# The lo parts of the plain feed-forward weight blocks by an accumulating DMA

## The chip, the cores and the metric

The kernel runs on one core of one Trainium2 chip. The metric is the device time of one launch in microseconds (us). The kernel before was timed in three runs. One further execution was recorded by the profiler; all durations in this document come from such recorded executions.

## The reference

The kernel computes one layer of an encoder on 512 tokens of width 1024, in float32. Only the end of the layer bears on the change:

```python
gates = jax.nn.sigmoid(gate_pre.reshape(B, S, N_BRANCHES, D_MODEL))
merged = (gates[:, :, 0] * (y_pool @ w_up_pool[l]) + gates[:, :, 1] * (y_attn @ w_up_attn[l])
          + gates[:, :, 2] * (y_rec @ w_up_rec[l]))
x = x + merged @ w_out[l]
h2 = rms_norm(x, norm2_g[l])
gu = h2 @ w_ffn_in[l]                     # (512, 1024) @ (1024, 2 * 2816)
x = x + (jax.nn.silu(gu[..., :FFN_HIDDEN]) * gu[..., FFN_HIDDEN:]) @ w_ffn_out[l]
```

Ahead of it stand a combined input projection, a pooling mixer, differential attention and a gated recurrence; behind it a last norm. The changed lines work in `h2 @ w_ffn_in` alone.

## The kernel before, in words

**Two-part numbers.** TensorE reads its operands in a shorter format (F32R). So every float32 operand w is split into hi, which is w rounded to that format, and lo = w - hi, and a product is made of three terms: hi x hi, hi x lo and lo x hi. For a weight block, `split_w` makes hi with a cast on ScalarE (line 183) and lo with a subtraction on VectorE (line 184). Both go into tiles `whi` and `wlo` of the pool `wsp`, which has three buffers for each name. A fourth split therefore waits until TensorE has read the buffer of the first.

**Feed-forward input.** The 2 x 2816 columns are worked off as 22 pairs of 128 columns, pair j being block j of the "up" half and block j of the "gate" half. Pair 0 is done plainly. Pairs 1 to 21 use Strassen's scheme in Winograd's form: a pair is a 2 x 2 arrangement of blocks, and 7 products stand in for 8. Of a pair's weights four *parts* are made, in this order:

- part 0: the first block as it stands, 128 x 1024 (`split_w`, the plain block);
- parts 1 and 2: sums of blocks (`sums`, three additions on VectorE, lines 261 to 265), split into `shi` and `slo` of another pool (lines 300 and 302);
- part 3: the second half of the second block as it stands, 128 x 512 (`split_w` again).

`ffn_pair_bodies` has the four bodies that use them: `first` (two products with part 0), `second` and `third` (two products each, with parts 1 and 2) and `fourth` (one product with part 3). Each product is 12 matmuls of 256 columns: four with hi, four with hi against the lo of the activations, four with lo. Its sums stand in PSUM banks `mm` and `rc`; ScalarE copies `mm` to `u` after the first product (line 1246) and again after the third (line 1264), VectorE makes the gate sum `g` (line 1275), ScalarE its silu (lines 1278 and 1285), and VectorE the result `hid` (line 1286). The product after a copy accumulates into the same bank, so it waits for the copy.

**Loads and order.** A pair's raw weights, 2 x 512 KB, are loaded by two DMAs of SyncE's queue into `raw` of the pool `wraw`, which has two buffers; so pair j + 2 is loaded when all that reads the raw weights of pair j is done. `Jobs.pump` writes loads and splits ahead of their use, up to four splits. A scheduler then sets the order on each engine; TensorE's order is fixed as written. Nothing else but these queues sets the order: each engine takes its instructions in turn and waits at the head for semaphores.

GpSimd (POOL) computes the few reciprocal roots of the norms and, in the feed-forward input, nothing.

Of the kernel before, what the change touches and what calls it, by code (L numbers as in the profile page):

```python
# [11 lines left out]
F32 = mybir.dt.float32  # L12
F32R = mybir.dt.float32r
U8 = mybir.dt.uint8
AF = mybir.ActivationFunctionType
ALU = mybir.AluOpType
PSUM = bass.MemoryType.PSUM

P = 128
# [3 lines left out]
KT = D // P  # L23
HEADS = 4
FFN = 2816
FT = FFN // P
# [50 lines left out]
def encoder_kernel(ctx: ExitStack, tc: tile.TileContext, x, norm1_g, w_in, pool_w, pool_scale,  # L77
# [3 lines left out]
    nc = tc.nc  # L81
# [82 lines left out]
    class Part:  # L164
# [9 lines left out]
        def split(self):  # L174
            self.hi, self.lo = split_w(self.view(self.chunk.raw), self.a, self.b, self.wpool, self.skip)
            self.chunk.left -= 1

    def split_w(view, a, b, wpool=None, skip=0):

        n, k = a * b, skip // 4  # L180
        hi, lo = ((wpool or wsp).tile([P, n if wpool else 1088], F32R, name=name)[:, k:k + n]
                  .rearrange("p (a b) -> p a b", a=a) for name in ("whi", "wlo"))
        nc.scalar.copy(out=hi, in_=view)  # L183
        LAST["wlo"] = nc.vector.tensor_tensor(out=lo, in0=view, in1=hi.bitcast(F32), op=ALU.subtract).ins  # L184
        return hi, lo

# [88 lines left out]
    class PairPart:  # L275

        wpool = None
# [15 lines left out]
        def sums_and_split(self):  # L293
            k = KT // 2
            if self.which in (1, 2):
                if self.chunk.sums is None:
                    self.chunk.add()
                view = self.chunk.sums[:, 2:4] if self.which == 1 else self.chunk.sums[:, 0:2]
                hi = LAST["ws"].tile([P, 2, k * P], F32R, name="shi")
                nc.scalar.copy(out=hi, in_=view)  # L300
                lo = LAST["ws"].tile([P, 2, k * P], F32R, name="slo")
                on_dve = nc.vector.tensor_tensor(out=lo, in0=view, in1=hi.bitcast(F32), op=ALU.subtract).ins  # L302
                FF.setdefault(f"s12_{self.chunk.name}", (on_dve,))
            elif self.which == 0:
                hi, lo = split_w(self.chunk.raw[:, 0], KT, P, None, self.skip)
                hi, lo = (t.rearrange("p k c -> p (k c)").rearrange("p (n x) -> p n x", n=2) for t in (hi, lo))
            else:
                hi, lo = split_w(self.chunk.raw[:, 1, k:], k, P, None, self.skip)
                hi, lo = (t.rearrange("p k c -> p (k c)").rearrange("p (n x) -> p n x", n=1) for t in (hi, lo))
            self.hi, self.lo = (t.rearrange("p n (k c) -> p n k c", c=P) for t in (hi, lo))  # L310
            self.chunk.left -= 1
# [237 lines left out]
    class First:  # L549
        wpool = None  # L550
# [51 lines left out]
    for i in range(3):  # L602
        for n, _ in enumerate(cols_mm(ps0[i], first[i], hT, KT, 0, 0, 256, i == 0)):
            if (i, n) in ((1, 5), (2, 5)):
                b = 1 + i
# [607 lines left out]
    class TilePart:  # L1213

        wpool = None
# [545 lines left out]
```

## Time and profile before

| | us |
|---|---|
| time, median of 3 runs (lowest to highest) | 885.27 (884.33 to 885.49) |
| the profiled execution's own time | 883.61 |
| its span, first to last instruction | 881.8 |
| PE (TensorE matmuls) busy | 869.9 |
| DVE (VectorE) busy | 658.6 |
| ACT (ScalarE) busy | 441.8 |
| POOL (GpSimd) busy | 19.0 |
| SyncE's DMA packets, share of the 16 DMA engines' span | 31.9% |

How to read it: the difference between span and time (1.8 us) lies around the first and the last instruction. Matmuls are pipelined, so a busy PE may still be one that could be fed faster. Idle time of an engine counts only where something that sets the end waits for it. In the rows, a line such as `L184` is that of the kernel before; `wlo<-raw,whi` means that the instruction reads `raw` and `whi` and writes `wlo`.

### The profile page before, as it was taken

The page shows a single profiled execution, that of the slowest core. Times are in us where ns is not written, and L with a number is a line of the kernel's source. Part 1 is how long each engine was busy: PE and PEld are TensorE (multiplying, and loading weights), DVE is VectorE, ACT ScalarE, POOL GpSimd, SP SyncE. Part 2 cuts the span into 40 slices and gives each one's busy share as a digit, 9 for nine tenths or more (in the row PEclk, how much of TensorE's full clock was granted, in tenths as well). Part 3 has the DMA queues.
Part 4 walks back from the last instruction along what each step waited for, and adds up shares of the span by engine and source line. Part 5 has one row for each costly group of instructions (what it writes and reads, how often), then busy time and mean ns, then how long its engine had stood idle before and what let it go on. Part 6 is the DMA issues. An engine that isn't in the chain of part 4 may idle for free.

```text
span 881.8 us, 13804 instructions
## 1 busy us (share of the span) xinstructions
PE 869.9 (99%) x5604; PEld 784.7 (89%) x5604; DVE 658.6 (75%) x992; ACT 441.8 (50%) x696; POOL 19.0 (2%) x35
## 2 busy tenths in 40 slices
PE   8999999999999999999999999999999999999996
PEld 7989988888998888888999898999999999988885
DVE  6788664845859765788777655997888888747996
ACT  6544333434646583444355425755555555533563
POOL 1000000000000000000000001000000000000001
PEclk9999999999999999999999999999999999999999
DMA  7330113124134114222431760153433443355002
GB/s 242 96 120 25 49 48 110 35 73 138 46 95 141 49 48 155 96 86 58 144 96 48 262 192 1 49 143 97 134 105 96 130 110 97 120 190 191 2 0 96
DMA packets 109579, 88.52 MB, mean 100 GB/s; under 512 B 2742, under 2 KB 98508, under 8 KB 109388
## 3 DMA queue, kind: packets, MB, share of 16 engines
q1 hardware_dynamic: 108924, 86.59, 31.9%
q8 instruction: 44, 0.72, 0.3%
q10 hardware_dynamic: 592, 1.05, 0.3%
q14 instruction: 19, 0.16, 0.1%
HBM read 85.54 MB, written 2.10 MB: 99 GB/s over the span
## 4 chain that ended last, share of the span: by engine, by line
PE 91%; DVE 4%; DMA 2%; issue 1%; ACT 1%; POOL 0%; SPq 0%; POOLq 0%; DVEq 0%; ACTq 0%
PE mm L90 62%; PE rc L90 25%; PE tp L90 2%; PE tp L98 2%; DMA raw<-in_w_out_dram 1%; DMA raw<-in_w_in_dram 1%; DVE wlo L184 1%; DVE hid L354 1%; DVE flo L354 1%; DMA xin<-in_x_dram 0%; DVE hrow L455 0%; DVE h_lo L472 0%; PE rc L98 0%; DVE slo L302 0%; DVE sums L261 0%
## 5 line engine op out<-in xcount | busy, mean ns | idle before, releaser
L183 ACT CAST whi<-raw 128x1024 fp32r<-128x1024 f32 (+1 forms) x134 | 128.7, 968 | 142.5 <-PE mm L90 98.7
L184 DVE TENSOR_TENSOR wlo<-raw,whi 128x1024 fp32r<-128x1024 f32 (+1 forms) x134 | 148.9, 1117 | 50.6 <-ACT whi L183 32.1
L90 PE MATMUL mm<-hT_hi,wlo 128*128 128x512 f32 (+1 forms) x380 | 92.3, 375 | 0.2 <-DVE wlo L184 0.2
L90 PE MATMUL mm<-hT_hi,whi 128*128 128x512 f32 (+1 forms) x380 | 91.6, 376 | 0.0
L90 PE MATMUL mm<-hT_lo,whi 128*128 128x512 f32 (+1 forms) x380 | 90.7, 374 | 0.0
L90 PEld LDWEIGHTS mm<-hT_lo,whi 128*128 128x128 f32 x380 | 66.6, 189 | 11.5
L90 PEld LDWEIGHTS mm<-hT_hi,whi 128*128 128x128 f32 x380 | 66.4, 189 | 11.7 <-ACT hT_hi L468 0.4
L90 PEld LDWEIGHTS mm<-hT_hi,wlo 128*128 128x128 f32 x380 | 66.2, 188 | 11.6 <-DVE wlo L184 0.4
L302 DVE TENSOR_TENSOR slo<-sums,shi 128x1024 fp32r<-128x1024 f32 x52 | 63.2, 1218 | 0.1
L300 ACT CAST shi<-sums 128x1024 fp32r<-128x1024 f32 x52 | 54.7, 1053 | 3.0 <-DVE sums L264 2.5
L261 DVE TENSOR_TENSOR sums<-raw 128x1024 f32<-128x1024 f32 x26 | 31.6, 1217 | 3.6 <-DMA raw<-in_w_in_dram 3.5
L860 DVE TENSOR_TENSOR kq<-kq,pyr 128x256 f32<-128x256 f32 x48 | 18.2, 420 | 18.3 <-PE rc L90 18.3
L90 PE MATMUL rc<-kq,kc 128*128 128x128 f32 x224 | 31.6, 284 | 0.0
L90 PEld LDWEIGHTS rc<-kq,kc 128*128 128x128 f32 x224 | 30.1, 191 | 1.5
L1002 ACT ACTIVATE s<-s,mx 128x512 f32<-128x512 f32 x32 | 23.1, 721 | 15.6 <-DVE mx L1000 15.4
L829 ACT COPY kc<-kq 128x512 f32<-128x512 f32 x28 | 18.6, 665 | 20.2 <-PE rc L90 12.6
L1275 DVE TENSOR_TENSOR g<-mm,g 128x256 f32<-128x256 f32 x21 | 8.9, 423 | 23.7 <-PE mm L90 23.7
L90 PE MATMUL mm<-y_hi,whi 128*128 128x512 f32 x96 | 26.6, 395 | 0.0
L90 PE MATMUL mm<-fhi,slo 128*128 128x256 f32 x168 | 26.1, 277 | 0.5 <-DVE slo L302 0.4
L90 PE MATMUL mm<-y_lo,whi 128*128 128x512 f32 x96 | 26.4, 393 | 0.0
L90 PE MATMUL mm<-fhi,shi 128*128 128x256 f32 x168 | 26.0, 277 | 0.1
L90 PE MATMUL mm<-y_hi,wlo 128*128 128x512 f32 x96 | 26.1, 391 | 0.0
(377 smaller groups left out, 1983.1 us busy)
## 6 DMA issues: line engine op xcount, KB each, us to landing
raw<-in_w_ffn_in_dram SPq DMA_DIRECT2D x44, 512.0 KB, 5.3
raw<-in_w_in_dram SPq DMA_DIRECT2D x34, 512.0 KB, 4.2
raw<-in_w_in_dram SPq DMA_DIRECT2D x13, 1024.0 KB, 5.2
raw<-in_w_ffn_out_dram SPq DMA_DIRECT2D x7, 1024.0 KB, 4.8
raw<-in_w_out_dram SPq DMA_DIRECT2D x4, 1024.0 KB, 9.6
xin<-in_x_dram SPq DMA_DIRECT2D x4, 512.0 KB, 4.1
raw<-in_w_up_rec_dram SPq DMA_DIRECT2D x2, 1024.0 KB
raw<-in_w_up_pool_dram SPq DMA_DIRECT2D x2, 1024.0 KB, 4.9
```

Source lines behind the costliest of these rows:

```text
L90: i = nc.tensor.matmul(out_, lhsT=lhsT, rhs=rhs, start=start, stop=stop, skip_group_check=chain)
L98: tc.keep_in_program_order(nc.tensor.transpose(out_, in_, idn))
L183: nc.scalar.copy(out=hi, in_=view)
L184: LAST["wlo"] = nc.vector.tensor_tensor(out=lo, in0=view, in1=hi.bitcast(F32), op=ALU.subtract).ins
L261: nc.vector.tensor_tensor(out=strided(sums, 0, [[2 * half, 2], [1, half]]), in0=strided(self.raw, 0, [[3 * half, 2], [1, half]]), in1=stri ...
L300: nc.scalar.copy(out=hi, in_=view)
L302: on_dve = nc.vector.tensor_tensor(out=lo, in0=view, in1=hi.bitcast(F32), op=ALU.subtract).ins
L354: last[0] = form(**kw).ins
L829: nc.scalar.copy(out=strided(kc, 0, [[2 * n, S // (2 * n)], [n, 2], [1, n]]), in_=strided(kq, 2 * S, [[2 * n, S // (2 * n)], [S + n, 2], [ ...
L860: nc.vector.tensor_tensor(out=xv, in0=xv, in1=tv, op=ALU.mult)
L1002: nc.scalar.activation(out=s, in_=s, func=AF.Exp, scale=-1.0, bias=mx[:, c:c + 1], accum_out=zz[:, i, c:c + 1])
L1275: on_dve = nc.vector.tensor_tensor(out=c["g"], in0=c["x"], in1=c["g"], op=ALU.add).ins
```

## The change

For pairs 5 to 21 the lo part of parts 0 and 3 is no longer subtracted on VectorE. ScalarE writes -hi into `wlo`, and a DMA of GpSimd's queue then adds the raw weights onto it in SBUF. Pairs 1 to 4, the sums of parts 1 and 2 and all other splits stay as they are.

```diff
-    def split_w(view, a, b, wpool=None, skip=0):
+    def split_w(view, a, b, wpool=None, skip=0, by_dma=False):
 
         n, k = a * b, skip // 4
         hi, lo = ((wpool or wsp).tile([P, n if wpool else 1088], F32R, name=name)[:, k:k + n]
                   .rearrange("p (a b) -> p a b", a=a) for name in ("whi", "wlo"))
         nc.scalar.copy(out=hi, in_=view)
+        if by_dma:
+            nc.scalar.activation(out=lo, in_=hi.bitcast(F32), func=AF.Copy, scale=-1.0)
+            nc.gpsimd.dma_start(out=lo.bitcast(F32), in_=view, accum_op=ALU.add)
+            return hi, lo
         LAST["wlo"] = nc.vector.tensor_tensor(out=lo, in0=view, in1=hi.bitcast(F32), op=ALU.subtract).ins
         return hi, lo
...
             elif self.which == 0:
-                hi, lo = split_w(self.chunk.raw[:, 0], KT, P, None, self.skip)
+                hi, lo = split_w(self.chunk.raw[:, 0], KT, P, None, self.skip, self.chunk.name in range(5, FT))
                 hi, lo = (t.rearrange("p k c -> p (k c)").rearrange("p (n x) -> p n x", n=2) for t in (hi, lo))
             else:
-                hi, lo = split_w(self.chunk.raw[:, 1, k:], k, P, None, self.skip)
+                hi, lo = split_w(self.chunk.raw[:, 1, k:], k, P, None, self.skip, self.chunk.name in range(5, FT))
```

That takes 34 subtractions from VectorE (17 of 128x1024, 17 of 128x512) and gives 34 instructions to ScalarE and 34 DMAs to GpSimd's queue. The order on TensorE and on SyncE's queue is the same as before. Line numbers behind the new lines are 4 higher.

On ScalarE, one pair in the steady part of the stage (`silu<-mm` is line 1285 before and 1289 after, the first `u<-mm` behind it the copy of line 1246 before and 1250 after) before:

```order
L183 CAST whi<-raw 128x1024
L1285 ACTIVATE silu<-mm 128x256
L1246 COPY u<-mm 128x256
L183 CAST whi<-raw 128x512
L1264 COPY u<-mm 128x256
```

The same place on ScalarE after the change, where `wlo<-whi` writes -hi:

```order
L183 CAST whi<-raw 128x1024
L1289 ACTIVATE silu<-mm 128x256
L185 ACTIVATE wlo<-whi 128x1024
L1250 COPY u<-mm 128x256
L183 CAST whi<-raw 128x512
L185 ACTIVATE wlo<-whi 128x512
L1268 COPY u<-mm 128x256
```

The longer new instruction stands between `silu` and the copy of `mm` that TensorE waits for; the shorter one stands behind the second cast.

On VectorE, the same stretch of one pair before (`sums` are the block sums of parts 1 and 2):

```order
L302 TENSOR_TENSOR slo<-sums,shi 128x1024
L184 TENSOR_TENSOR wlo<-raw,whi 128x1024
L261 TENSOR_TENSOR sums<-raw 128x2x512
L1286 TENSOR_TENSOR hid_5326<-silu,u 128x512
L184 TENSOR_TENSOR wlo<-raw,whi 128x512
L264 TENSOR_TENSOR sums<-sums,raw 128x512
L265 TENSOR_TENSOR sums<-sums,raw 128x512
```

And on VectorE after the change:

```order
L306 TENSOR_TENSOR slo<-sums,shi 128x1024
L265 TENSOR_TENSOR sums<-raw 128x2x512
L1290 TENSOR_TENSOR hid_5326<-silu,u 128x512
L268 TENSOR_TENSOR sums<-sums,raw 128x512
L269 TENSOR_TENSOR sums<-sums,raw 128x512
```

The two subtractions are gone and what stood behind them moves up; nothing else changes its place. The matmuls that read `wlo` now wait for the DMA, and SyncE's load of pair j + 2 waits for both accumulating DMAs of pair j as well, since they read its raw weights.

## Prediction

> **What bounds the kernel now.** I read the page first (busy times, chain), then a table by stretches of the stage that changes, then who waits there, then one pair in order of time, and last the DMAs.
>
> ```profile
> span 881.8 us, 13804 instructions
> PE 869.9 (99%) x5604; PEld 784.7 (89%) x5604; DVE 658.6 (75%) x992; ACT 441.8 (50%) x696; POOL 19.0 (2%) x35
> ...
> PE 91%; DVE 4%; DMA 2%; issue 1%; ACT 1%; POOL 0%; SPq 0%; POOLq 0%; DVEq 0%; ACTq 0%
> ```
>
> TensorE is busy 99% of the span and makes up 91% of the chain that ended last. VectorE's 4% of the chain must be looked for where the change is. The feed-forward input of pairs 5 to 21 lies at about 594 to 762 us; its table by stretches (columns: PE, PEld, DVE, ACT, POOL busy, granted clock, DMA share, GB/s), with the stage behind it as a fourth row:
>
> ```profile
> 594.00:650.00 56.00, 56.00 (x494) 55.91 (x494) 47.30 (x59) 32.39 (x54) 0.00 (x0) 1.00 0.42 114
> 650.00:706.00 56.00, 56.00 (x496) 56.00 (x496) 47.74 (x60) 32.37 (x53) 0.00 (x0) 1.00 0.40 112
> 706.00:762.00 56.00, 56.00 (x496) 56.00 (x495) 47.49 (x59) 32.20 (x54) 0.00 (x0) 1.00 0.39 115
> 762.00:800.00 38.00, 38.00 (x172) 31.55 (x171) 22.81 (x21) 15.46 (x18) 0.00 (x0) 1.00 0.43 155
> ```
>
> PE is busy 56.00 of 56.00 us in all three stretches, at full clock. VectorE is busy 142.5 of 168 us and ScalarE 97.0. In the list of waits of 594 to 762 us no row of its twelve has PE waiting; the others wait for PE:
>
> ```profile
> DVE g L1275 <- PE mm L90: 23.3, 17, 1.8
> ...
> ACT u L1246 <- PE mm L90: 8.2, 17, 0.5
> ACT whi L183 <- PE mm L90: 4.3, 17, 0.3
> ...
> DVE wlo L184 <- ACT whi L183: 0.2, 1, 0.2
> ```
>
> So this stage is bound by TensorE alone, and a lighter VectorE cannot shorten it. What is left to find out is whether the new way of making lo can make TensorE wait. One pair in order of time (start, us, engine, line):
>
> ```profile
> 647.89 0.62 PE L90 MATMUL mm<-fhi,wlo 128*128 128x256 f32 x4
> ...
> 648.09 1.05 ACT L183 CAST whi<-raw 128x1024 fp32r<-128x1024 f32 x1 [0.25 <-PE mm L90]
> ...
> 649.05 0.37 ACT L1285 ACTIVATE silu<-mm 128x256 f32<-128x256 f32 x1
> ...
> 649.18 1.23 DVE L184 TENSOR_TENSOR wlo<-raw,whi 128x1024 fp32r<-128x1024 f32 x1
> ...
> 649.90 0.37 ACT L1246 COPY u<-mm 128x256 f32<-128x256 f32 x1 [0.48 <-PE mm L90]
> ...
> 650.86 0.63 ACT L183 CAST whi<-raw 128x512 fp32r<-128x512 f32 x1 [0.58 <-PE rc L90]
> ...
> 651.07 0.62 PE L90 MATMUL mm<-fhi,shi 128*128 128x256 f32 x4
> ...
> 652.62 0.37 ACT L1264 COPY u<-mm 128x256 f32<-128x256 f32 x1 [1.14 <-PE mm L90]
> ...
> 653.38 0.69 DVE L265 TENSOR_TENSOR sums<-sums,raw 128x512 f32<-128x512 f32 x1
> ...
> 655.41 0.42 DVE L1275 TENSOR_TENSOR g<-mm,g 128x256 f32<-128x256 f32 x1 [1.34 <-PE mm L90]
> ...
> 657.61 1.05 ACT L183 CAST whi<-raw 128x1024 fp32r<-128x1024 f32 x1 [0.25 <-PE mm L90]
> ...
> 658.77 0.62 PE L90 MATMUL mm<-h_hi,wlo 128*128 128x256 f32 x4
> ```
>
> The cast of part 0 comes every 9.52 us (648.09, 657.61): one pair is 84 matmuls, 9.52 us. The cast at 648.09 waits for PE's last reads of a pair's part 3 (647.89), three splits back, so it is for the pair whose lo PE reads at 658.77, not for the pair that starts next. Call it pair C. Before, its lo was ready at 650.41, 8.4 us early.
>
> **The change part by part.**
>
> *VectorE, less.* In the groups of 590.5 to 752 us the removed instructions are two rows:
>
> ```profile
> L184 DVE TENSOR_TENSOR wlo<-raw,whi 128x1024 fp32r<-128x1024 f32 x17 | 20.8, 1225 | 0.0
> ...
> L184 DVE TENSOR_TENSOR wlo<-raw,whi 128x512 fp32r<-128x512 f32 x17 | 11.6, 682 | 0.0
> ```
>
> That is 32.4 us of busy time gone. It is worth 0: PE waits for nothing here, and VectorE's next wait, `g`, is for PE (655.41). The sums end some 1.9 us earlier and VectorE then idles 1.9 us longer.
>
> *ScalarE, more.* No row shows its negation from SBUF to SBUF; the nearest are an activation of 128x1024 and a scaled copy of 128x512:
>
> ```profile
> L449 ACT ACTIVATE hrow<-x 128x1024 f32<-128x1024 f32 x4 | 4.2, 1061 | 6.8 <-DVE x L1164 6.8
> ...
> L1366 ACT ACTIVATE x<-x,rstd 128x512 f32<-128x512 f32 x4 | 2.9, 720 | 3.9 <-POOL rstd L140 3.9
> ```
>
> I take 1.06 and 0.72: 17 x 1.78 = 30.3 us, ScalarE 127 of 168 us. Its places matter more. The long one comes behind `silu` (ends 649.42) and ends at 650.48, so the copy `u` ends at 650.85 instead of 650.27; PE overwrites that bank at 651.07. 0.22 us is left, the narrowest margin of the change. With the scaled copy's excess over the 512 cast (0.72 to 0.63, a seventh) the negation takes 1.21 and 0.07 us is left. At the near end back-to-back ScalarE instructions overlap (silu starts at 649.05, the cast ahead of it is listed until 649.14), which gives 0.1 to 0.2 us back. Cost 0. The short one, 651.49 to 652.21, ends ahead of the next copy, which waits for PE until 652.62: 0.
>
> *The accumulating DMA of part 0.* POOL is idle here (0.00 in the table), so it issues at about 650.5; PE reads lo at 658.77. It may take 8.3 us. Before has no accumulating transfer, none from SBUF to SBUF and none issued by POOL. Nearest rows (KB each, median us from issue to landing):
>
> ```profile
> raw<-in_w_ffn_in_dram SPq DMA_DIRECT2D x44, 512.0 KB, 5.3
> raw<-in_w_in_dram SPq DMA_DIRECT2D x34, 512.0 KB, 4.2
> raw<-in_w_in_dram SPq DMA_DIRECT2D x13, 1024.0 KB, 5.2
> raw<-in_w_ffn_out_dram SPq DMA_DIRECT2D x7, 1024.0 KB, 4.8
> ...
> out_dram<-x SPq DMA_DIRECT2D x4, 256.0 KB, 2.9
> ```
>
> It writes 512 KB but must read both 512 KB of raw and 512 KB of -hi. The low end is a plain 512 KB, 4.2 us; the high end two of the slower kind one after the other, 10.6 us. I take the row with as many bytes as are read, 1024 KB: 5.2 us, landing at 655.7, 3.1 us early. Cost 0; at the high end 2.3 us late.
>
> A rule bears on the doubling. The Trainium skill, Collectives: The Full Stack, section "The bandwidth ceiling: the fold count and why AG ≠ RS ≠ AR", says that an add in the DMA is itself free but needs two source reads on one ring, and so runs at half a copy's rate. By its figure of about 31 GB/s for each engine, halved over 16 engines, 512 KB would be an estimated 2.1 us beside the fixed part. No run here shows it; the sum would stay 0.
>
> *Part 3's DMA.* 256 KB, between 2.9 and 5.8 us; as a 512 KB row 4.2. Even begun only when part 0's has landed it ends at 659.9, and PE reads it two periods after 647.89, at 666.93. Cost 0.
>
> *The load two pairs on.* SyncE's load was released by the last sum (653.38 + 0.69 = 654.07) and is now released by part 3's DMA, at 659.9 at the latest. One period from 644.6 us (first line: busy tenths of the DMA engines in 40 slices):
>
> ```profile
> DMA  0000145999999999999940000000000000000002
> ...
> q1 hardware_dynamic: 2080, 1.05, 40.2%
> ...
> raw<-in_w_ffn_in_dram SPq DMA_DIRECT2D x2, 512.0 KB, 4.5
> ```
>
> The engines are idle in the second half of the period, where the accumulating DMAs now fall. A load issued at 659.9 lands about 4.5 to 5.3 us later, at 665.2; its first reader is the cast of 667.13 (657.61 + 9.52). Behind the waiting load SyncE has only later loads. Cost 0. In capacity: 0.79 MB accumulated is 1.57 MB read. At the loads' 114 GB/s at a share of 0.42 (271 GB/s when busy) that is 5.8 us, at the next stage's 155 at 0.43 (360 GB/s) 4.4 us; with the loads' 3.8 us, 8.2 to 9.6 of 9.52. It fits, but tightly.
>
> *POOL's queue.* 34 DMAs, in front of the last norm's four roots, which come some 100 us later: 0.
>
> *Sum:* 883.61 (profiled execution: span 881.8 and 1.8 around it) + 0 = 883.6. That execution stands 1.7 us below the median of the runs, 885.27, so I forecast the median, 885.3.
>
> **The rivals.**
>
> *The DMA lands late.* Slower. It decides from 8.3 us on. If s late, PE waits s at pair C. Pair D's split was started before that wait and its lo comes just as PE does; pair E's split waits for C's part 3 and is s late again. So every second pair pays: 9 x s. At 10.6 us, s = 2.3 and 9 x 2.3 = 21 us: 906. For it: three unknowns at once (accumulate, SBUF to SBUF, POOL). Against: 3.1 us of reserve.
>
> *POOL cannot prepare its DMA while VectorE works.* After the change VectorE runs without a gap from 649.2 (sums, hid, two sums: 1.22 + 3 x 0.68) to about 652.5 and is then idle until 655.41. A DMA held until 652.5 lands at 657.7 by my price, still in time, and part 3's behind it at 661.9; the load then lands at 667.2, 0.1 us late. So alone this costs next to nothing; it decides where the transfer itself takes over 6.3 us. With 7.5 us s is 1.2, 9 x 1.2 = 11 us: 896. The Trainium skill, SBUF — State Buffer, section "SBUF: two separate sides", states such a lock: GpSimd cannot write descriptors while VectorE runs an instruction in a 2-port mode. By its words two SBUF inputs alone block only a GpSimd instruction that reads SBUF. No run here shows it yet.
>
> *DMA engines run out.* If accumulating runs at half the loads' rate, 11.6 + 3.8 = 15.4 us a pair: 17 x 5.9 = 100 us, 985. The 40.2% row speaks against it; only the unknown rate for it.
>
> *ScalarE is late with `u`.* 0.22 us short becomes a wait: each 0.1 us over is 17 x 0.1 = 1.7 us; at 1.5 us for the negation 0.22 over, 3.7 us: 889.
>
> *Faster.* PE has no gap to close here; only shorter matmuls could do it, and no row shows VectorE slowing them. 883 at best.
>
> **How the numbers follow.** Forecast, no change: 0.70, own range 883.5 to 887.0 (0.2%, 1.8 us, is what can be told from no change). Late DMA 0.13; held by VectorE with a slow transfer 0.05; engines run out 0.04; ScalarE 0.04; faster 0.04. So faster 0.04, same 0.70, slower 0.26. The range goes up through ScalarE's case and the smaller half of the late ones (s up to 1.4, 9 x 1.4 = 12.6), to 898, and leaves out 0.15 or so.
>
> **What would show it.** Right: pair period still 9.52 us, PE busy 56.00 of 56.00, VectorE about 110 of 168 and ScalarE 127, DMA share 0.8 to 0.95, issue to landing of `wlo<-raw` below 8.3 us, load waits of SyncE on the DMA. Wrong: PE waiting for a DMA at the first `h_hi,wlo` of every second pair; PE waiting for `u`; or POOL spending microseconds on each DMA.

## The result and the profile after

The changed kernel takes 892.07 us (median of 4 runs, 890.65 to 892.86) against 885.32 us (884.33 to 885.49): a ratio of 1.0077, 95% interval 1.0063 to 1.0091. It is slower by 6.8 us. The time lies inside the stated range, but the forecast, no change, was wrong. The profiled execution is one of 892.86 us, the slowest of the four; what its profile loses is therefore somewhat more than the median does.

From the page of the changed kernel: its busy times, the chain by engine, the group of the instructions that issue the accumulating DMAs, and three DMA issues (KB each, median us from issue to landing):

```profile
span 891.1 us, 13880 instructions
PE 876.1 (98%) x5604; PEld 789.3 (89%) x5604; DVE 629.2 (71%) x958; ACT 466.0 (52%) x730; POOL 50.3 (6%) x69
...
PE 86%; DMA 6%; DVE 4%; ACT 2%; issue 1%; POOL 0%; POOLq 0%; ACTq 0%; SPq 0%; DVEq 0%
...
L186 POOL DMA_DIRECT2D wlo<-raw x34 | 29.8, 878 | 175.2 <-ACT u L1250 135.3
...
raw<-in_w_ffn_in_dram SPq DMA_DIRECT2D x44, 512.0 KB, 6.2
...
wlo<-raw POOLq DMA_DIRECT2D x17, 512.0 KB, 5.9
...
wlo<-raw POOLq DMA_DIRECT2D x17, 256.0 KB, 8.0
```

PE's share of the chain fell from 91% to 86%, and DMA's rose from 2% to 6%: somewhere the end now waits for transfers. The loads take 6.2 us instead of 5.3, and the smaller accumulating DMA is the slower one, 8.0 us for 256 KB. The table by stretches of the changed kernel's stage (columns as before: PE, PEld, DVE, ACT, POOL busy, granted clock, DMA share, GB/s):

```profile
594.00:650.00 56.00, 54.85 (x474) 54.48 (x473) 34.99 (x45) 37.99 (x61) 10.63 (x12) 1.00 0.77 172
650.00:706.00 56.00, 55.71 (x475) 54.73 (x475) 37.05 (x47) 39.46 (x63) 9.78 (x12) 1.00 0.83 180
706.00:762.00 56.00, 54.55 (x471) 53.76 (x470) 35.34 (x45) 37.78 (x60) 9.40 (x11) 1.00 0.87 189
```

PE, gapless before, is idle 2.9 us of 168 and gets through some 20 fewer matmuls in each stretch, still at full clock. The stretches end before the stage does now. Who waits there, in the list of waits of 590 to 780 us of the changed kernel (us in total, times, longest):

```profile
DVE sums L265 <- DMA raw<-in_w_ffn_in_dram: 18.5, 11, 3.2
...
ACT whi L183 <- DMA raw<-in_w_ffn_in_dram: 10.2, 12, 1.6
...
PEld mm L90 <- ACT u L1250: 2.8, 8, 0.9
...
PEld mm L90 <- DMA wlo<-raw: 2.4, 3, 1.3
...
PE mm L90 <- DMA wlo<-raw: 1.8, 2, 1.1
...
PE mm L90 <- ACT u L1250: 0.9, 2, 0.7
```

The first two rows are new: the cast and the sums, which used to find their weights long there, wait for the load. TensorE waits in two places: 8 times for the copy `u` behind that cast, and 3 times for a lo part (PE and PEld, its weight loads, list parts of the same waits). Where the time went, by the distance of each pair's first `fhi,shi` matmul from the next pair's (us, worked out from the order of time of the two profiled executions):

```
before 10.01 9.52 9.51 9.52  9.52 9.53 9.52  9.52 9.51 9.52 9.52  9.52  9.53 9.52  9.52  9.51 9.52
after  10.00 9.52 9.52 11.01 9.89 9.89 10.13 9.77 9.82 9.78 10.24 10.54 9.80 10.26 10.56 9.52 9.80
```

Before, from 593.46 to 755.78; after, from 594.81 to 764.86: 162.32 us became 170.05. So 7.7 of the span's 9.3 us arise in the stage; 1.3 us lie ahead of it, where the code is the same, and 0.2 us behind it.

### The profile page after: what moved, and what is told of

Read it like the earlier page. It is cut to its first block, busy times and chain, and to the rows that moved or that the text cites. A ratio compares the mean times of both kernels' runs of the same rounds, so it can differ in the third digit from the quotient of the medians.

```text
span 891.1 us, 13880 instructions
## 1 busy us (share of the span) xinstructions
PE 876.1 (98%) x5604; PEld 789.3 (89%) x5604; DVE 629.2 (71%) x958; ACT 466.0 (52%) x730; POOL 50.3 (6%) x69
## 3 DMA queue, kind: packets, MB, share of 16 engines
q0 software_dynamic: 4896, 13.37, 8.7%
q10 hardware_dynamic: 592, 1.05, 0.3%
## 4 chain that ended last, share of the span: by engine, by line
PE 86%; DMA 6%; DVE 4%; ACT 2%; issue 1%; POOL 0%; POOLq 0%; ACTq 0%; SPq 0%; DVEq 0%
PE mm L90 59%; PE rc L90 22%; PE tp L90 2%; DMA raw<-in_w_ffn_in_dram 2%; DMA wlo<-raw 2%; PE tp L98 2%; DMA raw<-in_w_out_dram 1%; DMA raw<-in_w_ffn_out_dram 1%; DVE wlo L188 1%; ACT whi L183 1%; PE rc L98 1%; DVE hid L358 1%; DVE hrow L459 0%; DVE flo L358 0%; DVE h_lo L476 0%
## 5 line engine op out<-in xcount | busy, mean ns | idle before, releaser
L188 DVE TENSOR_TENSOR wlo<-raw,whi 128x1024 fp32r<-128x1024 f32 (+1 forms) x100 | 116.5, 1173 | 51.4 <-ACT whi L183 31.5
L186 POOL DMA_DIRECT2D wlo<-raw x34 | 29.8, 878 | 175.2 <-ACT u L1250 135.3
L833 ACT COPY kc<-kq 128x512 f32<-128x512 f32 x28 | 18.6, 666 | 20.3 <-PE rc L90 12.6
L185 ACT ACTIVATE wlo<-whi 128x1024 fp32r<-128x1024 f32 (+1 forms) x34 | 28.6, 842 | 0.5
```

The source lines that it names most:

```text
L185: nc.scalar.activation(out=lo, in_=hi.bitcast(F32), func=AF.Copy, scale=-1.0)
L186: nc.gpsimd.dma_start(out=lo.bitcast(F32), in_=view, accum_op=ALU.add)
L833: nc.scalar.copy(out=strided(kc, 0, [[2 * n, S // (2 * n)], [n, 2], [1, n]]), in_=strided(kq, 2 * S, [[2 * n, S // (2 * n)], [S + n, 2], [ ...
```

## The experiments

**The theory (A in the expectations): the load is released too late.** There are two raw buffers, so the load of pair j + 2 goes where pair j lies. The accumulating DMA of part 3 now reads that buffer last, so the load can start only when it lands, and the next cast in that buffer only when the load does. This round has two pair periods, 2 x 9.52 = 19.04 us. One round of the changed kernel in order of time (start, us, engine, line):

```profile
701.79 1.05 ACT L183 CAST whi<-raw 128x1024 fp32r<-128x1024 f32 x1 [1.20 <-DMA raw<-in_w_ffn_in_dram]
...
704.36 0.87 POOL L186 DMA_DIRECT2D wlo<-raw  x1 [6.63 <-ACT u L1250]
...
705.81 0.87 POOL L186 DMA_DIRECT2D wlo<-raw  x1 [0.57 <-ACT wlo L185]
...
712.33 1.05 ACT L183 CAST whi<-raw 128x1024 fp32r<-128x1024 f32 x1 [1.58 <-DMA raw<-in_w_ffn_in_dram]
...
713.56 1.05 ACT L185 ACTIVATE wlo<-whi 128x1024 fp32r<-128x1024 f32 x1
...
714.50 0.36 ACT L1250 COPY u<-mm 128x256 f32<-128x256 f32 x1
...
714.92 0.74 PE L90 MATMUL mm<-fhi,shi 128*128 128x256 f32 x4 [0.73 <-ACT u L1250]
...
722.13 1.05 ACT L183 CAST whi<-raw 128x1024 fp32r<-128x1024 f32 x1 [0.85 <-DMA raw<-in_w_ffn_in_dram]
```

The casts of 701.79 and 722.13 use one buffer: 20.34 us apart, where 19.04 are to be had. The parts: 4.02 us to the issue of part 3's DMA (705.81), 9.2 until it lands (715.00), 0.2 until SyncE issues the load (715.19), and 6.9 until the cast of 722.13, which has waited for its half of the load. The cast stands at the head of ScalarE's queue, so a late load holds `silu`, the negation and the copy `u` behind it: the cast of 712.33 waits 1.58 us for its load, and at 714.92 PE waits 0.73 us for `u`. Over the fifteen rounds whose two casts both lie in the stage the distance is 19.04 twice, else 19.5 to 21.6, and 20.1 in the mean; before it is 19.04 in every one. (The last of the fifteen, the one of 21.6, ends at the first load of the next stage.)

The first wait of the stage is of another kind. A pair's cast starts on time at 620.88, and the accumulating DMA of its part 0 is issued at 623.46; it takes 9.4 us, the longest of the seventeen:

```profile
620.88 1.05 ACT L183 CAST whi<-raw 128x1024 fp32r<-128x1024 f32 x1 [0.30 <-PE mm L90]
...
623.46 0.87 POOL L186 DMA_DIRECT2D wlo<-raw  x1 [6.92 <-ACT u L1250]
...
632.87 0.74 PE L90 MATMUL mm<-h_hi,wlo 128*128 128x256 f32 x4 [1.15 <-DMA wlo<-raw]
```

The late release seems to have a hand in this too, though no run tests it by itself: the load that part 3's DMA held back was issued at 622.86, 0.6 us ahead of part 0's DMA. Of the seventeen DMAs of part 0 the three that took 8.6 us or more (9.4, 8.7 and 8.6) are the three that PE waited for, and each was issued 0.2 to 1.3 us behind a load; the ten that were issued ahead of the next load took 5.5 to 6.8 us.

The other theories: the transfers' traffic slows the stage whoever waits for it, ScalarE is late by its own added work (C), or the lo parts come late by themselves (B). The first four experiments ran on one chip beside the kernel before (median there 884.49 us), the other four on a second one (884.78).

**ScalarE's work without the DMA.** -hi is written as in the change, and VectorE adds the raw weights:

```diff
-            nc.gpsimd.dma_start(out=lo.bitcast(F32), in_=view, accum_op=ALU.add)
+            nc.vector.tensor_tensor(out=lo, in0=view, in1=lo.bitcast(F32), op=ALU.add)
```

> ScalarE's part alone: -hi is written by ScalarE as in the changed kernel, but the raw weights are added onto it by VectorE (34 additions where the 34 subtractions stood), so no DMA of GpSimd's is left. Theory A (two raw buffers: the load of pair j + 2 waits for the landing of part 3's accumulating DMA, the round of cast, negation, DMA, load, next cast takes 20 us where two pairs give 19.04) expects 885.3, within 0.1%. Theory B (lo itself lands too late for TensorE) expects 885.3 too. Theory C (the negation stands in front of the copy u that TensorE waits for) expects TensorE waits of 0.15 to 0.3 us at that copy in most pairs: 888 to 890.

Measured: 884.73 us, ratio 1.0 [0.999, 1.0009]. The middle stretch of its table:

```profile
650.00:706.00 56.00, 56.00 (x497) 56.00 (x496) 47.28 (x60) 40.43 (x65) 0.00 (x0) 1.00 0.40 112
```

ScalarE has all the work of the change (40.43 us in this stretch against 32.37) and PE has no gap. So ScalarE's extra work, at the place where the change puts it, costs nothing; the wait for `u` in the changed kernel comes from the late cast.

**A third raw buffer.** Pairs 6, 9, 12, 15 and 18 get their weights into a free part of another tile, so a load replaces pair j - 3 instead of j - 2; DMAs and traffic stay:

```diff
+            if self.where == "xr":
+                self.raw = FF["hid"][2][:, 4:8, :].rearrange("p a s -> p (a s)").rearrange(
+                    "p (c k x) -> p c k x", c=2, k=KT)
...
+        if name in range(6, 19, 3):
+            ch.where = "xr"
```

> The changed kernel with a third raw buffer for pairs 6 to 18: every third pair (6, 9, 12, 15, 18) is loaded into a part of the result tile that is written only from pair 20 on, so that a load waits for the pair three back. All transfers are the same. Theory A expects the loss gone as long as the third buffer works: a pair period of 9.52 us up to about pair 19, and 886 to 887.5 in all. Theory B expects no help: the accumulating DMAs are as slow as before, 891 to 893. Theory C: 888 to 892.

Measured: 885.11 us, 1.0003 [0.999, 1.0017].

```profile
650.00:706.00 56.00, 56.00 (x497) 56.00 (x496) 37.39 (x48) 40.42 (x65) 10.44 (x12) 1.00 0.87 198
```

PE has no gap at a DMA share of 0.87 (0.83 in this stretch of the changed kernel), and all casts are 19.04 us apart over two pairs. The accumulating DMAs are not much shorter than in the changed kernel (medians of 6.1 to 7.2 us, the longest of part 0 7.9): what has grown is the time that a round may take. That is what theory A says, though A had still expected a loss of 1 to 2 us.

**Part 0 alone by DMA.** Part 3 is subtracted on VectorE as before:

```diff
-                hi, lo = split_w(self.chunk.raw[:, 1, k:], k, P, None, self.skip, self.chunk.name in range(5, FT))
+                hi, lo = split_w(self.chunk.raw[:, 1, k:], k, P, None, self.skip)
```

> Only part 0 (the longer one, 17 DMAs of 512 KB) goes by the accumulating DMA; part 3's lo is subtracted on VectorE as before. Theory A: the load is released when part 0's DMA lands, some 8 us after the cast and not 13 after it, so the round of two pairs has 4 to 5 us to spare: 885.3 to 886. Theory B: part 0's lo is what TensorE needs first, and it is as late as before: 890 to 892. Theory C: the long negation still stands in front of the copy: 888 to 890.

Measured: 884.07 us, 1.0001 [0.999, 1.0013]; PE is busy 56.00 of 56.00. Its DMA issues in 594 to 762 us:

```profile
raw<-in_w_ffn_in_dram SPq DMA_DIRECT2D x30, 512.0 KB, 5.1
wlo<-raw POOLq DMA_DIRECT2D x17, 512.0 KB, 4.5
```

Alone, the accumulating 512 KB take 4.5 us instead of 5.9, and the loads 5.1 instead of 7.2 in the stage.

**The same DMAs from another source.** They add a part of the residual's tile, which nobody overwrites here, instead of the raw weights, so they load the engines alike but no longer hold the raw buffer:

```diff
-            nc.gpsimd.dma_start(out=lo.bitcast(F32), in_=view, accum_op=ALU.add)
+            other = LAST["x2"][:, 0, 0:n].rearrange("p (a b) -> p a b", a=a)
+            nc.gpsimd.dma_start(out=lo.bitcast(F32), in_=other, accum_op=ALU.add)
```

> The same accumulating DMAs, but they add a tile that has nothing to do with the weights (the residual), so the results are other ones; the same bytes move by the same queue, and the load of pair j + 2 no longer waits for these DMAs, only for the casts and VectorE's sums, as in the kernel before. Theory A: 885.3 to 886.5, loads still lengthened by the traffic, but issued some 10 us earlier in the round. Theory B (lo lands too late, or the DMA engines are overloaded): 890 to 893. Theory C: 888 to 890.

Measured: 885.04 us, 1.0005 [0.9993, 1.0016]. Its middle stretch, then (in a fence of its own) its DMA issues:

```profile
650.00:706.00 56.00, 56.00 (x497) 56.00 (x496) 37.39 (x48) 40.42 (x65) 10.44 (x12) 1.00 0.91 192
```

```profile
raw<-in_w_ffn_in_dram SPq DMA_DIRECT2D x30, 512.0 KB, 8.2
wlo<-x POOLq DMA_DIRECT2D x16, 512.0 KB, 5.5
wlo<-x POOLq DMA_DIRECT2D x17, 256.0 KB, 7.3
```

This run tells traffic from release. The accumulating transfers are nearly as slow as in the changed kernel, the loads even slower (8.2 us), the DMA engines busier (0.91), and PE has no gap. Long transfers alone cost nothing; long transfers in a closed round do. The median of part 0's DMA is not much lower here (5.5 us), but none takes more than 5.6, where the changed kernel has three of 8.6 to 9.4: each load is now issued some 1.8 us behind part 0's DMA and none just ahead of it. So this run takes away both waits of PE, that for `u` and that for lo, and does not part them.

**The changed kernel again**, on the second chip, with no edit.

> The changed kernel itself once more, beside the next three on one chip: 890 to 893 by every theory, with the cast of part 0 coming every 20 us for two pairs.

Measured: 891.72 us, 1.0068 [1.0047, 1.0088]. Its profiled execution, one of 889.04 us, parts the two waits: no wait for a lo part is in it (the longest DMA of part 0 takes 8.0 us), PE waits for `u` six times, and the stage still takes 165.77 us, 3.4 more than before. The rounds were expected at 20 us; the first six are of 19.04 to 19.07 us, the others of 18.8 to 21.1, and the mean is 19.5.

**Part 3 alone by DMA**, the mirror of the run above (the last argument dropped in part 0's call):

> Only part 3 (17 DMAs of 256 KB) goes by the accumulating DMA; part 0's lo is subtracted on VectorE. Theory A: the same wait of the load on part 3's landing as in the changed kernel, but nothing of GpSimd's queue ahead of it, so it lands about 3 to 4 us after its issue and not 8, and the round of two pairs takes 4 + 4 + 6 = 14 us of the 19.04: 885, within 0.15%. A theory D, that any wait of SyncE's load on part 3's DMA costs, however short: 888 to 892.

Measured: 885.82 us, 1.0006 [0.9995, 1.0017], PE without a gap. A DMA issue, and apart from it a row of SyncE's waits in 590 to 762 us:

```profile
wlo<-raw POOLq DMA_DIRECT2D x17, 256.0 KB, 3.3
```

```profile
SPq L258 <- DMA wlo<-raw: 125.6, 15, 10.7
```

SyncE's queue waits for part 3's DMA nearly as long as in the changed kernel (133.1 us there), and it does no harm: the order of the round is the same, but 256 KB take 3.3 us instead of 8.0. So neither the wait as such nor part 3's place in it costs anything; the landing times of two accumulating DMAs and a load that share the engines do.

**A plain copy through the same queue**, of the same bytes, without the addition:

```diff
-            nc.gpsimd.dma_start(out=lo.bitcast(F32), in_=view, accum_op=ALU.add)
+            nc.gpsimd.dma_start(out=lo.bitcast(F32), in_=view)
```

> The same DMAs of GpSimd's queue with the same waits, but as plain copies, without the addition (lo is the raw weight then). The destination is not read: a 4096-byte packet should take about 159 ns, as the plain ones of the kernel before, and not 328. Theory A: the DMAs land 2 to 4 us sooner, the load is starved for half as long, the round takes 15 to 17 us of 19.04: 885, within 0.15%. Theory D: 888 to 892. If GpSimd's way of issuing, and not the second read, made the DMAs slow, 889 to 892.

Measured: 884.8 us, 0.9997 [0.9987, 1.0007]. Its queue and DMA issues in 594 to 762 us (queue, packets, MB, share of the engines' time):

```profile
q0 software_dynamic: 3808, 13.37, 19.8%
...
wlo<-raw POOLq DMA_DIRECT2D x16, 512.0 KB, 2.9
wlo<-raw POOLq DMA_DIRECT2D x17, 256.0 KB, 2.3
```

The same row of the changed kernel in 594 to 770 us:

```profile
q0 software_dynamic: 4896, 13.37, 44.1%
```

For the same 13.37 MB the addition takes 44.1% of 176 us instead of 19.8% of 168 (77.6 against 33.3 us, 2.3 times). In the packet records an accumulating 4096-byte packet lasts 328 ns in the median, a plain one 159. With plain copies the round closes in time.

**Release by halves.** The two raw tiles are kept and used again instead of being given back, so each half of a load waits only for that half's readers: the first half, which the cast reads, for part 0's DMA and the sums. Buffers and transfers are those of the change:

```diff
-            self.raw = (LAST[self.where] if self.where else wraw).tile([P, 2, KT, P], F32, name="raw")
+            if getattr(self, "name", None) in range(7, FT):
+                self.raw = FF["raws"][self.name % 2]
+            else:
+                self.raw = (LAST[self.where] if self.where else wraw).tile([P, 2, KT, P], F32, name="raw")
+                if getattr(self, "name", None) in (5, 6):
+                    FF.setdefault("raws", {})[self.name % 2] = self.raw
```

> The changed kernel with the same two raw buffers and the same transfers, but the buffers are kept and not handed back between pairs, so that each half of a load waits for the readers of its own half: the first 512 KB for part 0's DMA, the second for part 3's. Theory A: the first half, which the next cast needs, is released some 8 us after the cast; the second half is released as late as before but needed only by the sums and the second cast. The round of the first half takes 8 + 6 = 14 us, that of the second 13 + 4 = 17 us of 19.04: 885 to 886. If the load's length and not its release were what is late, 889 to 892.

Measured: 885.91 us, 1.0009 [0.9996, 1.0022]. Its middle stretch, and its DMA issues:

```profile
650.00:706.00 56.00, 56.00 (x497) 56.00 (x496) 37.34 (x48) 40.57 (x66) 10.44 (x12) 1.00 0.85 194
```

```profile
raw<-in_w_ffn_in_dram SPq DMA_DIRECT2D x30, 512.0 KB, 4.9
wlo<-raw POOLq DMA_DIRECT2D x17, 512.0 KB, 4.7
wlo<-raw POOLq DMA_DIRECT2D x17, 256.0 KB, 4.7
```

The loss is gone, within the interval, with two buffers and all 34 DMAs, at a share of 0.85. The landings came down as well (part 3's from 8.0 to 4.7 us). We put that down to fewer packets meeting, since the halves of a load are now issued some 2 to 5 us ahead of the next pair's accumulating DMAs; no run tests this by itself.

Each of the seven edits lengthens what the round may take, takes the DMA out of it or lightens its transfers, and each brings the time back to that of the kernel before, within its interval. None beats it; PE has no gap there to close.

## Why the prediction was right or wrong

- *VectorE, less: worth 0.* Right. VectorE is busy 107.4 us of 168 in the changed kernel (forecast about 110), and the time did not fall.
- *ScalarE, more: cost 0.* Right in effect, by the first experiment. The negation takes 1.05 and 0.63 us (1.06 and 0.72 taken); ScalarE is busy 115.2 of 168 us, where 127 was forecast. The margin of 0.22 us at `u` held as long as the cast itself was on time; the rival "late with `u`" showed its sign, the waits for `u`, but not its cause.
- *The accumulating DMA of part 0: 5.2 us, cost 0.* About right alone (4.5) and a little low in company (5.9), but not cost 0: three of the seventeen took 8.6 to 9.4 us, past the 8.3 us at which the prediction said it would turn late, and cost 2.3 us together. The price by bytes read was a good guess: an accumulating packet lasts twice a plain one, 328 against 159 ns. The trace agrees with the Trainium skill (Collectives: The Full Stack, "The bandwidth ceiling: the fold count and why AG ≠ RS ≠ AR"), by which the second source read halves the rate.
- *Part 3's DMA: 2.9 to 5.8 us, end at 659.9 at the latest.* Wrong in size. In the round shown it lands 13.2 us after part 0's cast, where 11.8 (648.09 to 659.9) was called the latest; the median landing is 8.0 us. The step took a price from a row in which the DMA engines served little else. Alone the same DMA took 3.3 us (part 3 by itself), inside the price.
- *The load two pairs on: lands 1.9 us early, cost 0.* This is the step that failed. The mechanism stood there, release by part 3's DMA and the next cast's deadline, but its terms were added from undisturbed rows: 11.8 + 5.3 = 17.1 us of 19.04. Measured: 13.2 + 0.2 + 6.9 = 20.3. The load was priced at 4.5 to 5.3 us and takes 7.2 in the median of the stage, because the next pair's accumulating DMAs run beside it. The prediction's own times had them meet: the load at 659.9, the next pair's DMA of part 0 at 650.5 + 9.52 = 660.0; each was still priced as if alone.
- *In capacity it fits, but tightly.* Right: 0.77 to 0.87 busy (forecast 0.8 to 0.95), so the rival "DMA engines run out" is out. But this line should have been a warning: with 8.2 to 9.6 us of transfers in a period of 9.52, most of them are likely to meet others unless their order keeps them apart, as in the release by halves; the step just above used undisturbed times.
- *The rivals.* "The DMA lands late" came true in part: the wait at lo is there, in 3 pairs of 17 and not in every second one, and the first of them struck a split that had started on time. Its waits are 2.3 us of the stage's loss in the first profile and nothing in the second. A late load stood in one rival alone, where POOL is held up by VectorE: there it was 0.1 us late and put at next to nothing. "POOL cannot prepare its DMA while VectorE works" itself did not show. The row of line 186 of the changed kernel (duration in ns, min/median/max):

```profile
L186 POOL DMA_DIRECT2D wlo<-raw x34: 872/872/1065, 594.0 to 756.4; - x34
```

  POOL takes 872 ns for its DMA, 1065 at most, though VectorE is busy two thirds of the time. So the lock that the Trainium skill states (SBUF — State Buffer, "SBUF: two separate sides") for VectorE's 2-port mode is not seen beside this kernel's float32 sums and subtractions.

The sum was 0. With the measured round it would have come near: 20.1 us in the mean instead of 19.04 is 1.1 us over; 17 pairs are 8.5 rounds, and 8.5 x 1.1 = 9 us, where the stage shows 7.7. That the time lies inside the stated range is in good part luck: the range was carried up to 898 for ScalarE's case and for late lo parts, not for a load that comes late.

Of the stage's 7.7 us, PE's waits make up 4.8 us, read from start to start since the modelled ends hide a part of them (2.3 at lo parts, 2.5 at `u`). In the ten stalls that end inside the stage the first matmul after the stall is followed by the second 0.22 us later and not 0.11: 1.1 us together. The other 1.8 us are a slower pace of the matmuls, told below. Why a stall has these two effects stays open, and so does what fixes which pair is the first to be late.

## What to carry to other kernels

When a DMA becomes a reader of a buffer that is loaded in turn, its landing is a term of a closed round (first use, last reader, release, load, first use): write the round down with all its terms and compare the sum with the number of buffers times the period. Price transfers that overlap in that round together, not each from a row where it ran alone: in the changed kernel (DMA share 0.77 to 0.87) they took 1.3 to 2.4 times as long. The share alone does not tell: with the release by halves, at 0.85, they took 4.7 to 4.9 us. Where the round did not close, a third buffer, a release by halves, or moving only one of the two parts repaired it here.

## What the runs showed of the hardware

- Accumulating costs the DMA engines twice a copy's time: 328 against 159 ns for a packet of 4096 bytes within SBUF, and POOL is busy 872 ns with issuing an accumulating DMA against 546 with a plain one (medians of 34 each).
- The two queues seem to take turns by packets, not by bytes. In the packet records of the changed kernel, from 707.0 to 709.0 us of the round shown, 60 accumulating packets of 4096 bytes start and 60 of the load's, of 512 bytes; from 709.5 to 712.5 us, with those of part 0 through and those of part 3 not yet begun, the load starts 235 to 330 in each 0.5 us. So a queue with small packets starves beside one with large slow ones; the run from another source shows it as 8.2 us for a load of 5.1.
- In the changed kernel PE's matmuls of 256 columns came every 117.8 ns instead of 113.3 for three stretches of 7 to 30 us (633 to 663 us, for one), at a granted clock of 1.00. Of the six changes of pace, five stand at a stall and one, at 696.9 us, does not. What sets the pace was not tried.
